# Down of both feed-forward blocks as seven products of quarter blocks, in a decoder layer on one Trainium2 core

## The chip, the cores and the metric

The kernel runs on one core of one Trainium2 chip. The core has five engines with an instruction queue each: TensorE (PE, matmuls; PEld is its loading of weights), VectorE (DVE), ScalarE (ACT), GpSimd (POOL) and SyncE (SP), which here issues most DMA transfers. Matmuls read on-chip memory (SBUF) and add up in PSUM, which has eight banks of 128x512 fp32. The metric is device time in microseconds (us), median of several runs; one further execution is recorded by the hardware profiler.

## The reference

One decoder layer on 1024 tokens of width 1024, all in fp32. A feed-forward block (ffn1), a token mixer and a second feed-forward block (ffn2) follow each other, each with a residual and a layer norm:

```
def swiglu(x, w_gate, w_up, w_down):
    return (jax.nn.silu(x @ w_gate) * (x @ w_up)) @ w_down

x = layer_norm(ALPHA * x + 0.5 * swiglu(x, ffn1_w_gate, ffn1_w_up, ffn1_w_down), ln1_g, ln1_b)
mix = token_mixer(x, ...)
x = layer_norm(ALPHA * x + mix, ln2_g, ln2_b)
x = layer_norm(ALPHA * x + 0.5 * swiglu(x, ffn2_w_gate, ffn2_w_up, ffn2_w_down), ln3_g, ln3_b)
```

The inner width of a feed-forward block is 2816 = 22 · 128. The token mixer (an mLSTM branch and an RWKV branch, merged by gates and multiplied by w_out) is left as it is.

## The kernel before

**Products.** Every fp32 product is made of three matmuls in a rounded fp32 format (`mm3`, L148): each operand is split into a high part (a cast on ACT, L131) and a low part (a subtraction on POOL or DVE, L135), and high·high, high·low and low·high are added in PSUM. A matmul has a 128x128 stationary and a 128x512 moving operand.

**Gate stage.** For each of the 22 blocks f of 128 inner columns, gate and up are made together as seven products of quarter blocks (`gate_up`, L272): four loads of weights (`rw`, a ring of 8 buffers), four subtractions between them (`weights`, L254; `tw` on DVE, L256), seven splits (ACT and POOL), 7·4·3 = 84 matmuls of 128x512 into three PSUM accumulators X, Y, Z (tags g, b, c), and additions on DVE that read PSUM (L277) and SBUF (L300, L304). The order of the seven is X, Y, X, Y, Z, Y, Z; what DVE reads of Y after the second product must be read before the fourth begins. h, the activated inner values, goes to DRAM in two stores per f (L285), with the inner dimension as rows and the tokens as columns. The first f of ffn1 (`gate_first`) also transposes x and makes its block sums (`put_sums`, L219) for four pairs of 128-token rows; pairs 0 and 1 before the first half of f = 0, pairs 2 and 3 between its two halves.

**Down stage.** `down_all` (L351) makes the 1024x1024 result in three passes over 128-token row blocks: 0 to 2, 3 to 5, 6 and 7. In each pass and for each f it loads a strip of h (`hr`, 128 x n·128) and two halves of a row block of w_down (`rw`), splits all three (ACT high, DVE low; split operands are in the ring `wr`), and runs 6n matmuls for n row blocks into the six or four accumulators of the pass. Half way through a pass the rows of x are loaded for the residual (tiles `u`, 128x1024, L378). At a pass's end DVE adds the accumulators to them (L386) and the rows are normalized (`layer_norm`, L396: statistics L399, centring on ACT L403, times g L404, a reciprocal root in small steps L161 to L165, times the root and plus b L413): those of passes one and two late, beside the next pass; rows 6 and 7 after the last matmul. At ffn1 each normalized row is also transposed on PE (L174) for the token mixer's products; at ffn2 it is the output. The same function makes w_out's product in the mixer (with 8 blocks instead of 22).

**What sets the order.** The kernel is written as a sequence of tile operations; a list scheduler of the framework orders each engine's instructions when the program is built. On the chip each engine works through its list in order and waits at an instruction whose inputs or buffers are not ready. SP too issues its DMAs in order, so a DMA that waits for a buffer holds up those behind it.

## Time and profile before

| | us |
|---|---|
| median of 3 runs | 3199.72 (3197.56 to 3206.72) |
| the profiled execution | 3204.13 |
| its span | 3202.1 |
| mean granted clock of PE in it | 0.977 |
| ffn1: first down matmul to last | 462.52 to 716.72 |
| ffn2: first down matmul to last | 2944.76 to 3187.88 |
| from ffn2's last down matmul to the end of the span | 14.2 |

All times of the profile are microseconds from the start of the span. Rows of the timeline and of groups name an engine, a line of the code and an operation as output<-inputs, with buffer numbers left out; `xN` counts instructions; in brackets stands how long the engine was idle before, and which instruction ended that. In the chain, which is followed back from the last instruction of the span, each row is a start, a duration and what took that time. Matmuls are pipelined, so the durations of single ones overlap; the chain's pieces do not.

### The profile page before, as it was taken

What the parts mean: (1) busy time and instruction counts of PE and PEld (TensorE: products, weight loads), DVE (VectorE), ACT (ScalarE), POOL (GpSimd) and SP (SyncE); (2) the same over time, 40 slices, a digit from 0 to 9 for tenths busy, and PEclk for the clock granted to TensorE, in tenths of its full rate; (3) what the DMA queues carried; (4) which work ended last, traced back from release to release, by engine and by line L of the source; (5) the groups of instructions that cost most, each with busy time, mean ns of one, the idle gap of its engine ahead of it and who ended that gap; (6) DMA issues with size and microseconds to landing.
All of it is one profiled execution on the core that took longest, in us unless ns stands there. A gap on an engine that the chain in (4) does not pass through costs nothing. (4 is left out here: it accounts for less than half of the span.)

```text
span 3202.1 us, 45591 instructions
## 1 busy us (share of the span) xinstructions
PE 3056.9 (95%) x15888; PEld 2486.7 (78%) x15888; DVE 1909.5 (60%) x4812; ACT 1098.2 (34%) x1836; POOL 761.8 (24%) x819
## 2 busy tenths in 40 slices
PE   7999999999899999999999999999999799999997
PEld 6888878877677777787877777777777688888886
DVE  7444435583657667758575856567648844444557
ACT  4333324453312222313131322186424433333444
POOL 4444420011212222222221222210000344442000
PEclk9999999999889999999999999999999899999999
DMA  4323236672222232322222323285586333223665
GB/s 128 97 83 86 79 107 215 200 220 72 64 54 77 69 77 60 80 56 75 68 72 64 85 67 99 70 273 175 171 270 196 102 87 89 83 86 112 215 202 186
DMA packets 497389, 373.81 MB, mean 117 GB/s; under 512 B 110941, under 2 KB 415751, under 8 KB 497159
## 3 DMA queue, kind: packets, MB, share of 16 engines
q1 hardware_dynamic: 488135, 357.26, 37.7%
q0 software_dynamic: 4608, 8.39, 1.0%
q10 hardware_dynamic: 4416, 5.24, 0.5%
q8 instruction: 125, 2.05, 0.3%
q14 instruction: 105, 0.86, 0.1%
HBM read 287.43 MB, written 83.36 MB: 116 GB/s over the span
## 5 line engine op out<-in xcount | busy, mean ns | idle before, releaser
L151 PE MATMUL psg<-xT,wf 128*128 128x512 f32 x2352 | 638.7, 408 | 1.6 <-DVE h L1108 0.9
L151 PEld LDWEIGHTS psg<-xT,wf 128*128 128x128 f32 x2352 | 428.0, 191 | 78.0 <-ACT wf L131 1.3
L131 ACT CAST wr<-rw 128x512 fp32r<-128x512 f32 x444 | 273.2, 621 | 489.8 <-PE psc L151 271.2
L135 DVE TENSOR_TENSOR wr<-rw,wr 128x512 fp32r<-128x512 f32 x312 | 215.6, 696 | 193.9 <-ACT wr L131 188.3
L151 PE MATMUL psa<-xT,w 128*128 128x512 f32 x1200 | 318.1, 407 | 7.5 <-DVE pj L480 4.7
L135 POOL TENSOR_TENSOR wr<-tw,wr 128x512 fp32r<-128x512 f32 x176 | 231.4, 1316 | 273.7 <-ACT wr L131 273.7
L135 POOL TENSOR_TENSOR wr<-rw,wr 128x512 fp32r<-128x512 f32 x132 | 175.9, 1333 | 432.8 <-DMA rw<-in_ffn_w_up_dram 239.2
L151 PEld LDWEIGHTS psa<-xT,w 128*128 128x128 f32 x1200 | 223.2, 192 | 59.3 <-DVE pj L480 9.4
L151 PE MATMUL psg<-wr,wr 128*128 128x512 f32 x936 | 250.8, 395 | 13.8 <-DVE wr L135 8.7
L151 PE MATMUL psb<-xq,wr 128*128 128x512 f32 (+1 forms) x1104 | 256.2, 381 | 4.7 <-DVE e L277 2.4
L151 PE MATMUL psc<-xq,wr 128*128 128x512 f32 (+1 forms) x1104 | 256.9, 380 | 1.6 <-POOL wr L135 1.6
L277 DVE TENSOR_TENSOR e<-psb,e 128x512 f32<-128x512 f32 (+1 forms) x138 | 92.1, 668 | 270.5 <-PE psb L151 270.5
L151 PE MATMUL psb<-wr,wr 128*128 128x512 f32 x936 | 247.2, 391 | 0.0
L151 PEld LDWEIGHTS psb<-xq,wr 128*128 128x128 f32 x1104 | 201.7, 188 | 45.5 <-issue 2.1
L151 PEld LDWEIGHTS psc<-xq,wr 128*128 128x128 f32 x1104 | 201.8, 188 | 41.5 <-POOL wr L135 1.8
L151 PEld LDWEIGHTS psg<-wr,wr 128*128 128x128 f32 x936 | 173.9, 188 | 58.9 <-DVE wr L135 16.2
L131 ACT CAST wr<-tw 128x512 fp32r<-128x512 f32 x176 | 108.9, 621 | 307.0 <-PE psb L151 217.9
L151 PEld LDWEIGHTS psb<-wr,wr 128*128 128x128 f32 x936 | 175.5, 188 | 36.3
L135 POOL TENSOR_TENSOR w<-raw,w 128x512 fp32r<-128x512 f32 (+1 forms) x51 | 65.5, 1297 | 488.3 <-ACT w L131 409.6
L135 POOL TENSOR_TENSOR wf<-rawf,wf 128x512 fp32r<-128x512 f32 x98 | 129.7, 1339 | 169.4 <-ACT wf L131 153.8
L151 PE MATMUL psc<-wr,wr 128*128 128x512 f32 x624 | 159.2, 390 | 0.0
L758 POOL TENSOR_SCALAR S<-S,PC 128x128 f32<-128x128 f32 x120 | 80.4, 670 | 292.8 <-DVE S L760 177.3
(345 smaller groups left out, 5104.5 us busy)
## 6 DMA issues: line engine op xcount, KB each, us to landing
rw<-in_ffn_w_down_dram SPq DMA_DIRECT2D x264, 256.0 KB
rawf<-in_w_in_dram SPq DMA_DIRECT2D x98, 256.0 KB
rw<-in_ffn_w_gate_dram SPq DMA_DIRECT2D x88, 256.0 KB
rw<-in_ffn_w_up_dram SPq DMA_DIRECT2D x88, 256.0 KB
h<-e SPq DMA_DIRECT2D x80, 256.0 KB
hr<-h SPq DMA_DIRECT2D x88, 192.0 KB
raw<-in_w_in_dram SPq DMA_DIRECT2D x50, 256.0 KB
rw<-in_w_out_dram SPq DMA_DIRECT2D x48, 256.0 KB
```

Of the source, the lines that this page charges most:

```text
L131: nc.scalar.copy(hi, src)
L135: eng.tensor_tensor(lo, src, hi.bitcast(F32), op=ALU.subtract)
L151: self.nc.tensor.matmul(out, a[u], b[v], start=first and i == 0, stop=last and i == 2, skip_group_check=more)
L277: add = lambda o, a, b: nc.vector.tensor_tensor(o, a[:, cs], b, op=ALU.add)
L758: nc.gpsimd.tensor_scalar(S1, S, pcn, None, op0=ALU.mult)
```

## The change

Down becomes seven products of quarter blocks. h (1024 tokens by 2816) and w_down (2816 by 1024) are each cut into 2x2 quarters; a product m goes over i = 0 to 10, a pair of 128-row blocks of the inner dimension, with a stationary of 128x512 (four token blocks) and a moving operand of 128x512, 12 matmuls per i. Four of the operands on each side are sums of quarters. These are made ahead, in the gate stage, by `sums`: for each i four loads of 128x512 (ring `pr`, 4 buffers), four DVE operations and four stores to DRAM. The sums of w are written into the program at f < 11, those of h at f > 11, when the h blocks that they need exist; the last of h stands at the start of `down_seven`. The products accumulate in three sets of four PSUM banks, X, Y, X, Z, Z, Y, Y; DVE adds each into the residual tiles at its end, twelve operations after the first product and four after each other one. All eight `u` tiles are loaded at i = 3 of the first product. Rows 0 to 3 are complete after the fifth product and normalized in the sixth and seventh; rows 4 to 7 after the seventh.

In `gate_first` the block sums of x of pairs 2 and 3 are put between the products of the first half of f = 0, two steps ahead of each. The constants of the token mixer (`consts2`) are loaded at the start of the sixth product rather than early in the first pass. The tiles `f` and `bnd3` of the mixer are no longer reserved during ffn1's down. `tw` has 5 buffers instead of 6, `wr` 12 in the down stages; w_out's product still goes through `down_all`.

```diff
-    RING = {"rw": (8, F32), "tw": (6, F32), "wr": (14, F32R), "e": (14, F32), "hr": (4, F32)}
+    RING = {"rw": (8, F32), "tw": (5, F32), "wr": (14, F32R), "e": (14, F32), "pr": (4, F32)}
...
+        def pr(ps, i, first):
+            for _ in range(2 if between and i else 0):
+                next(between, None)
+            self.prod(ps, ws[i], cmb[i], first, cs)
...
-        self.gate_up(cmb, 0, ws, hD, 0, 256)
-        pair(2)
-        pair(3)
+        steps = (s for p in (2, 3) for s in self.put_steps(cmb, p, *A[p], self.ring("tw"), "ad"))
+        self.gate_up(cmb, 0, ws, hD, 0, 256, steps)
+        for _ in steps:
+            pass
         self.gate_up(cmb, 0, ws, hD, 256, 512)
+        self.sums(pre, "w", self.I[f"{pre}_w_down"][0], 0)
...
+            if f < NH:
+                self.sums(pre, "w", wd, f)
+            elif f > NH:
+                self.sums(pre, "h", hD, f - NH - 1)
...
+    def sums(self, pre, kind, src, i):
...
+        q11, q12, q21, q22 = (self.ring("pr") for _ in range(4))
+        for t, r, c in ((q11, 0, 0), (q12, 0, 1), (q21, 1, 0), (q22, 1, 1)):
+            nc.sync.dma_start(t, self.quarter(src, kind, r, c, i))
+        if kind == "h":
+            tt_(q22, q21, q22, op=ALU.add)
+            tt_(q21, q11, q21, op=ALU.subtract)
+            tt_(q11, q22, q11, op=ALU.subtract)
+            tt_(q12, q12, q11, op=ALU.subtract)
+            out = q22, q11, q21, q12
+        else:
+            tt_(q11, q12, q11, op=ALU.subtract)
+            tt_(q12, q22, q12, op=ALU.subtract)
+            tt_(q22, q22, q11, op=ALU.subtract)
+            tt_(q21, q21, q22, op=ALU.subtract)
+            out = q11, q22, q12, q21
+        for m, t in enumerate(out):
+            nc.sync.dma_start(self.SD[key][(m * NH + i) * P:(m * NH + i + 1) * P, :], t)
...
+        self.parts = [(A(0, 0), B(0, 0)), (S(2), T(2)), (A(0, 1), B(1, 0)), (S(1), T(1)), (S(4), B(1, 1)),
+                      (S(3), T(3)), (A(1, 1), T(4))]
...
+    def down_seven(self, pre, src, hD, ln_cb, hooks, ahead):
...
+        self.sums(pre, "h", hD, NH - 1)
+        acc = {}
+        for m in range(7):
+            name = "XYXZZYY"[m]
+            first = m in (0, 1, 3)
+            if first:
+                acc[name] = [self.ps(t) for t in ("ggbb" if name == "Y" else "ccad")]
+            ps = acc[name]
+            for i in range(NH):
+                raws = ahead.pop(0) if ahead else self.part_load(m, i)
...
+                for t in raws:
+                    d = self.ring("wr"), self.ring("wr")
+                    self.split(t, *d, lo_eng="dve")
+                    ds.append(d)
+                if (m, i) == (0, 3):
+                    hooks[0]()
+                    for tt in range(8):
+                        t = self.unit()
+                        nc.sync.dma_start(t, src[tt * P:(tt + 1) * P, :])
+                        y.append(t)
+                if (m, i) == (5, 0):
+                    hooks[1]()
+                if i % 5 == 4 and late:
+                    late.pop(0)()
+                for j in range(4):
+                    self.mm3(ps[j], self.cut(ds[0], ALL, slice(j * P, (j + 1) * P)), ds[1], first and i == 0, i == NH - 1,
+                             not first)
+            for j in range(4):
+                c11, c12 = (y[j][:, c * 512:(c + 1) * 512] for c in range(2))
+                c21, c22 = (y[4 + j][:, c * 512:(c + 1) * 512] for c in range(2))
+                if m == 0:
+                    for t in (c12, c21, c22):
+                        stt(t, t, ALPHA, ps[j], op0=ALU.mult, op1=ALU.add)
+                elif m == 2:
+                    stt(c11, c11, ALPHA, ps[j], op0=ALU.mult, op1=ALU.add)
+                else:
+                    t = {1: c12, 3: c22, 4: c12, 5: c22, 6: c21}[m]
+                    tt_(t, t, ps[j], op=ALU.add)
+                if m == 4:
+                    late.append(lambda tt=j: ln_cb(tt, y))
+        for j in range(4):
+            ln_cb(4 + j, y)
```

Three places show what the scheduler makes of it. Lines of the changed kernel are its own: L396 to L399 are the four operations of a sum of w, L402 its stores, L447 the `u` loads, L418 the operands of the products, L466 an addition of a product to a residual tile, L523 to L537 the normalization; L291, L319, L323 and L269 are what L277, L300, L304 and L256 were.

SP at the start of ffn1's down, before (a strip of h and two halves of w_down are one f's operands):

```order
L346 DMA hr_4142<-h_77 128x384
L442 DMA vnat_3952<-in_m_conv_w_dram 64x128
L348 DMA rw_4143<-in_ffn_w_down_dram 128x512
L348 DMA rw_4144<-in_ffn_w_down_dram 128x512
L346 DMA hr_4178<-h_77 128x384
L378 DMA u_4232<-in_x_dram 128x1024
L378 DMA u_4234<-in_x_dram 128x1024
L348 DMA rw_4179<-in_ffn_w_down_dram 128x512
L348 DMA rw_4180<-in_ffn_w_down_dram 128x512
L346 DMA hr_4214<-h_77 128x384
L378 DMA u_4236<-in_x_dram 128x1024
```

The same queue now, from the stores of the last h sum to the fifth pair of operands of the first product (`rw_4238`, `rw_4239`):

```order
L402 DMA sum_ffn1h<-pr_4110 128x512
L402 DMA sum_ffn1h<-pr_4111 128x512
L447 DMA u_4210<-in_x_dram 128x1024
L447 DMA u_4212<-in_x_dram 128x1024
L447 DMA u_4214<-in_x_dram 128x1024
L447 DMA u_4216<-in_x_dram 128x1024
L447 DMA u_4218<-in_x_dram 128x1024
L447 DMA u_4220<-in_x_dram 128x1024
L447 DMA u_4222<-in_x_dram 128x1024
L447 DMA u_4224<-in_x_dram 128x1024
L418 DMA rw_4238<-h_77 128x512
L418 DMA rw_4239<-in_ffn_w_down_dram 128x512
```

The three `u` loads that stood among the operands are eight in a row, after the stores and ahead of the fifth pair.

DVE in the gate stage of ffn1, f = 3 from its second product on, before (`e` are the additions of the gate stage, `tw` the differences of weights for the next f):

```order
L277 TENSOR_TENSOR e_948<-psb_954,e_946 128x512
L256 TENSOR_TENSOR tw_1212<-rw_1208,rw_1204 128x512
L277 TENSOR_TENSOR e_949<-psb_954,e_946 128x512
L256 TENSOR_TENSOR tw_1213<-rw_1206,tw_1211 128x512
L277 TENSOR_TENSOR e_950<-psc_955,e_949 128x512
L256 TENSOR_TENSOR tw_1360<-rw_1354,rw_1352 128x512
L277 TENSOR_TENSOR e_951<-psb_954,e_946 128x512
```

The same stretch now (`pr` are the blocks of a sum of w):

```order
L291 TENSOR_TENSOR e_997<-psb_1003,e_995 128x512
L269 TENSOR_TENSOR tw_1292<-rw_1289,tw_1291 128x512
L396 TENSOR_TENSOR pr_1599<-pr_1600,pr_1599 128x512
L397 TENSOR_TENSOR pr_1600<-pr_1602,pr_1600 128x512
L291 TENSOR_TENSOR e_998<-psb_1003,e_995 128x512
L398 TENSOR_TENSOR pr_1602<-pr_1602,pr_1599 128x512
L269 TENSOR_TENSOR tw_1293<-rw_1289,rw_1285 128x512
L399 TENSOR_TENSOR pr_1601<-pr_1601,pr_1602 128x512
L291 TENSOR_TENSOR e_999<-psc_1004,e_998 128x512
L269 TENSOR_TENSOR tw_1294<-rw_1287,tw_1292 128x512
L291 TENSOR_TENSOR e_1000<-psb_1003,e_995 128x512
```

Between the readings of PSUM now stand the operations of a sum; a second sum follows in the same f, and f = 1 to 4 of ffn1 have two each.

DVE after the last product of ffn2, before:

```order
L386 SCALAR_TENSOR_TENSOR u_28380<-u_28380,psg_27967 128x512
L386 SCALAR_TENSOR_TENSOR u_28380<-u_28380,psg_27968 128x512
L399 BN_STATS lnst_28699<-u_28380 128x6 x2
L386 SCALAR_TENSOR_TENSOR u_28382<-u_28382,psb_27969 128x512
L400 BN_AGGR lnmv_28698<-lnst_28699 128x2
L386 SCALAR_TENSOR_TENSOR u_28382<-u_28382,psb_27970 128x512
```

And now:

```order
L466 TENSOR_TENSOR u_26730<-u_26730,psg_26930 128x512
L466 TENSOR_TENSOR u_26732<-u_26732,psg_26931 128x512
L523 BN_STATS lnst_28617<-u_26730 128x6
L466 TENSOR_TENSOR u_26734<-u_26734,psb_26932 128x512
L466 TENSOR_TENSOR u_26736<-u_26736,psb_26933 128x512
L524 BN_AGGR lnmv_28616<-lnst_28617 128x2
L523 BN_STATS lnst_28625<-u_26732 128x6
```

Two residual tiles were finished there, and now four are; 25 such rows of DVE stood from the first of these to the end of the program, and 49 stand there now.

More of the change, by code (lines that the diff above doesn't have):

```diff
@@ L22 @@
 NF = DFF // P
+NH = NF // 2
 ALPHA = 2.0 ** 0.25
@@ L225, in put_sums @@
         tt_(a2[0], a1[0], a2[0], op=ALU.subtract)
+        yield
         put(1, a1[1])
         tt_(a1[0], s1, a1[0], op=ALU.subtract)
+        yield
         put(2, a1[0])
+        yield
         put(3, a2[0])
         tt_(a1[1], a1[1], a1[0], op=ALU.subtract)
+        yield
         put(4, s1)
+        yield
         put(5, a2[1])
+        yield
         put(6, a1[1])
+    def put_sums(self, *args):
+        for _ in self.put_steps(*args):
+            pass
     def prod(self, ps, w, x, first, cs):
@@ L334, in gate_rest @@
             if f == NF - 1:
-                ahead = [self.row_load(wd, hD, 0, 3, i) for i in range(2)]
+                self.down_parts(pre, hD)
+                ahead = [self.part_load(0, i) for i in range(2)]
             if f == 0:
@@ new lines, in part_load @@
+    def part_load(self, m, i):
+        raws = [self.ring("rw") for _ in range(2)]
+        for t, part in zip(raws, self.parts[m]):
+            self.loaded = self.nc.sync.dma_start(t, part(i))
+        return raws
+    def down_seven(self, pre, src, hD, ln_cb, hooks, ahead):
+        nc = self.nc
+        stt, tt_ = nc.vector.scalar_tensor_tensor, nc.vector.tensor_tensor
+        y, late, ahead = [], [], list(ahead)
+        self.sums(pre, "h", hD, NH - 1)
[8 more added lines that the diff above has]
+                raws = ahead.pop(0) if ahead else self.part_load(m, i)
+                if (m, i) == (6, 6):
+                    self.held = self.loaded
+                ds = []
+                for t in raws:
[30 more added lines that the diff above has]
+            ln_cb(4 + j, y)
@@ L343, in row_load @@
     def row_load(self, wd, hD, t0, n, f):
-        hr, raws = self.ring("hr", n * P), [self.ring("rw") for _ in range(2)]
+        hr, raws = self.ring("pr", n * P), [self.ring("rw") for _ in range(2)]
         self.nc.sync.dma_start(hr, hD[f * P:(f + 1) * P, t0 * P:(t0 + n) * P])
@@ L372, in down_all @@
                     hook()
-                if (f % 3 == 2 if nf == NF else f % 2) and late:
+                if f % 2 and late:
                     late.pop(0)()
@@ L1169, in build @@
             gx.enter_context(net.shared("gx", ("xT",)))
-            gw.enter_context(net.shared("gw", [t for t in net.GLOBAL if t != "xT"]))
-            with net.phase("A", UB=6, side="right"):
+            gw.enter_context(net.shared("gw", ("raw", "w", "rawf", "wf")))
+            with net.phase("A", UB=8, side="right"):
                 net.wp = net.sp
-                net.down_all(ins["ffn1_w_down"][0], NF, x, h1, fin1, hook1, ahead)
+                net.down_seven("ffn1", x, h1, fin1, (hook1, net.consts2), ahead)
         middle(net, ins, x1T, x1D)
@@ L1202, in build @@
             xs.close()
-            with net.phase("F", UB=6, side="right"):
-                gb3.extend(rows("ln3"))
-                net.down_all(ins["ffn2_w_down"][0], NF, x2D, h2,
-                             lambda tt, y: net.layer_norm(tt, y, *gb3, lambda t: nc.sync.dma_start(out[0, row(t), :], y[t])),
-                             None, ahead)
+            with net.phase("F", UB=8, side="right"):
+                net.down_seven("ffn2", x2D, h2,
+                               lambda tt, y: net.layer_norm(tt, y, *gb3, lambda t: nc.sync.dma_start(out[0, row(t), :], y[t])),
+                               (lambda: gb3.extend(rows("ln3")), lambda: None), ahead)
         gx.close()
```

34 lines of the change are left out of this document (23 added, 11 removed).

## The prediction

> **What bounds the kernel now.** I read the page's busy shares first, then the chain of work that ended last, then tables of busy time by stage.
>
> ```profile
> PE 3056.9 (95%) x15888; PEld 2486.7 (78%) x15888; DVE 1909.5 (60%) x4812; ACT 1098.2 (34%) x1836; POOL 761.8 (24%) x819
> ```
>
> TensorE (PE) is busy 95% of the span, so matmuls set the time nearly everywhere. The table by stage shows where they do not (start:end, length, then busy time of PE, PEld, DVE, ACT, POOL, the granted clock, DMA share, GB/s):
>
> ```profile
> 7.00:55.00 48.00, 36.25 (x236) 32.84 (x237) 41.37 (x63) 23.55 (x43) 15.00 (x13) 0.93 0.47 143
> 80.00:400.00 320.00, 320.00 (x1413) 264.98 (x1412) 134.19 (x184) 100.09 (x168) 152.07 (x118) 1.00 0.30 86
> 470.00:500.00 30.00, 30.00 (x134) 24.48 (x133) 13.84 (x27) 11.60 (x21) 0.00 (x0) 1.00 0.85 284
> 462.52:716.72 254.20, 249.95 (x1106) 203.39 (x1107) 164.80 (x299) 121.60 (x222) 11.80 (x11) 0.99 0.68 215
> 2480.00:2540.00 60.00, 41.58 (x241) 33.20 (x242) 56.09 (x101) 24.76 (x42) 16.32 (x10) 0.86 0.34 109
> 2944.76:3187.88 243.12, 240.98 (x1057) 197.46 (x1055) 148.51 (x279) 109.40 (x198) 0.00 (x0) 1.00 0.64 210
> ```
>
> In the gate stage (80 to 400) PE has no idle time. The two down stages, 254.2 and 243.1 us, are PE-bound but for 4.3 and 2.1 us. The head (7 to 55) and the passage from w_out to the second gate stage (2480 to 2540) are VectorE's: DVE 41.4 of 48 and 56.1 of 60 us. The pace of a matmul is read from the chain, since the groups' means of 390 ns overlap:
>
> ```profile
> 2583.16 2.72 PE psg L151 x12
> ...
> 3182.45 1.36 PE psg L151 x6
> ```
>
> Both rows give 0.2267 us for one 128x512 matmul.
>
> **What the change removes.** Each ffn's down needs 8·2·22·3 = 1056 matmuls now and 7·11·4·3 = 924 afterwards. That is 264 fewer, 264 · 0.2267 = **-59.9 us**, all of it on the path. The sums are made against the profiled execution (3204.13 us, span 3202.1), 4.4 us above the median of 3199.72; the shift is then applied to the median.
>
> **What it adds: the eight u loads (+11, +5).** All rows of x are now loaded together early in the first product, ahead of the next operands in SP's queue; before, they went in threes between operands, half a pass in. These are the rows around the end of the first gate stage:
>
> ```profile
> 458.82 2.58 ACTq L285 DMA_DIRECT2D h<-e  x2
> ...
> 462.52 3.23 PE L151 MATMUL psg<-wr,wr 128*128 128x512 f32 x6 [3.13 <-ACT wr L131]
> ```
>
> PE idles 3.13 us before 462.52; call that idle time's start, 459.4, the gate stage's end, zero. The last h is issued by +2.0 (458.82 + 2.58). The last block sums need it, and behind them in SP's order stand their four stores, then the u loads, then the fifth pair of operands (i = 4). I use landings of 2.5 us after the issue, from the middle of these pieces of the chain (2.25 and 2.91 for loads; a store under load took 5.69):
>
> ```profile
> 2387.37 5.69 DMA mgD<-v
> ...
> 3125.53 2.25 DMA hr<-h
> ...
> 3136.22 2.91 DMA rw<-in_ffn_w_down_dram
> ```
>
> So h is in DRAM at +4.5, its four blocks are loaded at +8.5, the sums are done at about +12, and SP reaches the fifth pair at about +16. Ahead of it from +8 on are 4.2 MB of u, 1.0 MB of lng and lnb and 1.0 MB of stores. At the 284 GB/s of 470 to 500 they take 22 us. PE starts at +3.1 and has four pairs, 4 · 2.72 = 10.9 us of work: it needs the fifth at +14. If the pair landed 2.5 us after its issue, the wait would be 4 to 5 us; if all bytes go first at 284 GB/s, 16. I take **11**, nearer to the second, since the queue stands in that order. At ffn2 eight pairs (21.8 us) are loaded ahead and there is no gap before the stage: **5** (0 to 8).
>
> **The tails (+12, +9).** The left half of rows 4 to 7 gets its last part from the seventh product, so four rows are normalized after the last matmul, where two are now.
>
> ```profile
> 3185.88 1.37 DVE L386 SCALAR_TENSOR_TENSOR u<-u,psg 128x512 f32<-128x512 f32 x2 [2.23 <-PE psg L151]
> 3186.36 1.52 PE L151 MATMUL psb<-wr,wr 128*128 128x512 f32 x6
> 3187.17 1.28 DVE L399 BATCH_NORM_STATS2 lnst<-u 128x6 f32<-128x512 f32 x2
> ...
> 3193.03 0.16 DVE L164 SCALAR_TENSOR_TENSOR rst<-rst,lnv 128x2 f32<-128x2 f32 x1
> ...
> 3195.60 2.48 DVE L413 SCALAR_TENSOR_TENSOR u<-u,lnr,lnb 128x1024 f32<-128x1024 f32 x2
> 3196.92 1.54 SPq L1206 DMA_DIRECT2D out_dram<-u  x2
> ```
>
> Now DVE is dense from 3185.88 to 3198.08, 12.2 us. Afterwards stand four evictions (4 · 0.63), seven statistics (0.63 each), four final steps of 1.24 (L413, 2.48 for two), four products with g of the same size, and two root chains, 20 steps of 0.16 (0.2 with the gap behind each): 2.5 + 4.4 + 5.0 + 5.0 + 4 = 20.9, about 21. That is +9 at ffn2, hidden by nothing. At ffn1 the same rows are waited for by PE:
>
> ```profile
> 716.72 5.61 PE L151 MATMUL psg<-xT,wf 128*128 128x512 f32 x24
> ...
> 726.02 1.09 PE L174 MATMUL psa<-ident,u 128*128 128x128 f32 x4 [3.69 <-DVE u L413]
> ...
> 731.02 4.25 PE L151 MATMUL psa<-xT,w 128*128 128x512 f32 x15
> ```
>
> PE's order keeps the same 24 matmuls as cover and puts the transposes of all four rows before the next products: 9 of normalization and two more rows of transposes, about 2.5 each less overlap (726.02 to 731.02 for two), **+12** (8 to 14).
>
> **Block sums in the gate stage (+6, +6).** Each sum is four loads, four DVE subtractions of 128x512 and four stores. The order puts those of w at two per f for about four f's of each ffn; those of h come at one per f. What such an operation costs beside POOL (the first two rows are groups of 80 to 440, then the timeline):
>
> ```profile
> L277 DVE TENSOR_TENSOR e<-psb,e 128x512 f32<-128x512 f32 x57 | 39.4, 692 | 123.3 <-PE psb L151 123.3
> L304 DVE SCALAR_TENSOR_TENSOR e<-e,e 128x512 f32<-128x512 f32 x19 | 25.0, 1318 | 0.7
> ```
> ```profile
> 155.24 0.52 SPq L285 DMA_DIRECT2D h<-e  x1
> 155.30 1.30 POOL L135 TENSOR_TENSOR wr<-rw,wr 128x512 fp32r<-128x512 f32 x1 [1.41 <-ACT wr L131]
> 155.85 1.30 DVE L304 SCALAR_TENSOR_TENSOR e<-e,e 128x512 f32<-128x512 f32 x1
> 156.63 0.37 SPq L243 DMA_DIRECT2D rw<-in_ffn_w_gate_dram  x1
> ```
>
> L277 reads PSUM and takes 0.69. L304 reads SBUF twice, begins while POOL works (155.30 to 156.60) and ends only at 157.15: 0.55 us behind POOL's end. A sum costs 0.69 with POOL idle, 1.3 behind it, about 1.0 on average, since POOL is busy 152 of 320 us.
>
> [...]
>
> The `pr` ring has four buffers, one sum's worth, so sums form a loop: store issued (0.52), landed (2.5), two loads issued (0.74), landed (2.5), three subtractions (3.0), other DVE rows between (1.2): 10.5 us a turn. Two per f leave 84 · 0.2267 / 2 = 9.5. DVE takes its rows in order, so evictions wait behind a late sum, and PE behind them; an eviction has 2.0 us to spare (a product of 2.72 less 0.69). Eight turns 1 us too long, less 2 spare, make **+6** per ffn. Bounds: 8.5 a turn (2.25 landings, 0.69 a subtraction) costs nothing; 5.69 for the store and 1.77 a subtraction, as below, gives 16 and 50 per ffn. I stay by the load rows, which are 256 KB like these. The h sums, at one per f, have room: 0 (to 4).
>
> **The passage to ffn2 (+6).** Eight to ten w sums stand there among DVE's rows, where DVE is the bound.
>
> ```profile
> 2530.49 1.77 DVE L256 TENSOR_TENSOR tw<-rw,rw 128x512 f32<-128x512 f32 x1
> ```
>
> At 0.69 to 1.77 each they cost 6 to 17, less the 3.9 us in which DVE idles: 2 to 13, and 6 is nearest to the shorter rows, as POOL works only 16.3 of the 60.
>
> **The rest.** In the head the parts of x of pairs 2 and 3 move between products, which fills PE's gaps (48 - 36.3 us), and four sums are added to a busy DVE: -1 (-5 to +4). Evictions go from 16 to 36 per ffn, all but twelve between products on other banks; the twelve take 7.4 us against 6.8 of operands already split: about +1, and two fewer rows of transposes inside ffn1's down give that back. The normalization of rows 0 to 3 stalls PE as now (4.3 and 2.1 us of idle).
>
> **Sum:** -59.9 + 16 + 21 + 12 + 6 - 1 = **-5.9**: 3198 for the profiled execution, **3194** against the median.
>
> **Rivals.**
> *Faster: the loads and sums hide.* If a turn is below 9.5 us (landings at 2.25, subtractions finding POOL idle), the 12 us go; if the fifth pair lands soon after its issue, 8 of the 16. That gives 3194 - 20 = 3174. For it: DMA is at 0.30 of its share in the gate stage, and PE never waited there. Against it: the loop has no spare buffer.
> *Slower: the sums meet POOL.* If the three subtractions of a turn take 1.77 each, as at 2530.49, a turn is 12.8 us and each ffn loses 8 · 3.3 - 2 = 24 instead of 6: 3194 + 36 = 3230. It turns the sign from about 11.5 us a turn. For it: L304's row, and POOL as long busy as ever; against it: L256, also with two SBUF inputs, runs at 0.69 because it starts as POOL ends.
>
> ```profile
> L256 DVE TENSOR_TENSOR tw<-rw,rw 128x512 f32<-128x512 f32 x35 | 24.2, 692 | 39.6 <-POOL wr L135 39.6
> ```
>
> *The change doesn't do what it says:* the products run under the pace, for want of split operands. Each i needs two casts and two subtractions for twelve matmuls, where three of each stand now for 18; DVE is busy 165 of 254 us in the first down stage. So it could only happen where rows 0 to 3 are normalized beside it, in products six and seven. At 0.6 us lost in each of their 22 i's of both ffns it would be 26 us: 3220.
>
> **Chances.** Forecast 0.44 (3182 to 3206), faster rival 0.34, slower rival 0.18, pace 0.04. About 0.3%, 9.6 us, is what a measurement of this kernel can tell from no change; faster by more means below 3190.1, which is the faster rival and a fifth of the forecast's case: 0.43. Within: 0.36. Slower: 0.21. The range, 3164 to 3222, leaves out the lower end of the faster rival and more than half of the slower one, about 0.2.
>
> **What would show it.** Right: PE's pace of 1.36 per six in both down stages, which shrink by some 20 us each; one wait of PE for a DMA of rw some 14 us after each gate stage begins to be down; DVE dense for about 21 us after the last matmul; PE periods of about 21 us instead of 19.05 in four f's of each gate stage, DVE's L277 waiting behind sums that wait for DMA. Wrong: PE still 100% busy in 80 to 160, no wait at the fifth pair, or subtractions near 1.7 us. The term most likely to be mis-sized is the turn of the sums, then the u loads.

## The result, and the profile after

The changed kernel takes **3314.4 us** (median of 4 runs, 3314.08 to 3326.53) against 3198.64 (4 runs, 3197.05 to 3206.72): a ratio of **1.0354**, 95% interval 1.0333 to 1.0376. It is slower by 3.5%. The forecast was 3194 with a range up to 3222, so the time lies far outside, on the side that was given 0.21. The profiled executions are not the median ones: that of the changed kernel, with a span of 3324.7 us, is the slowest of its four, so 122.6 us more than in the profile before have to be found where the medians differ by 115.8.

Two rows of the page, the busy times and a group of PE by line and tile (matmuls of gate and up that go to the accumulator Y; ffn2 has further ones under another operand's name):

```profile
PE 3054.4 (92%) x15624; PEld 2474.3 (74%) x15624; DVE 2048.0 (62%) x4940; ACT 1067.3 (32%) x1750; POOL 778.6 (23%) x819
...
L154 PE MATMUL psb<-xq,wr 128*128 128x512 f32 (+1 forms) x1104 | 280.9, 406 | 63.8 <-DVE e L291 61.8
```

The 264 matmuls are gone (15888 to 15624), and yet PE is busy as long as before (3056.9): the matmuls that are left got slower, by some 57 us in all (an estimate: 3054.4 against 3056.9 less the 59.9 that 264 matmuls took). And the group of `psb` has 63.8 us of idle time before it, 61.8 of them ended by DVE's reading of PSUM (L291). Before, this was 4.7 us for the same 1104 matmuls. The table by stage (columns as in the prediction) shows the same:

```profile
80.00:400.00 320.00, 297.65 (x1263) 241.41 (x1262) 169.84 (x221) 90.56 (x152) 141.29 (x106) 0.97 0.51 157
2100.00:2200.00 100.00, 84.25 (x413) 66.66 (x412) 45.22 (x130) 43.58 (x66) 11.93 (x15) 0.91 0.56 175
```

From 80 to 400 PE was busy for all of the 320 us and made 1413 matmuls; now it makes 1263 and idles 22 us. The second row is a stretch of the token mixer, which the prediction had not looked at.

With marks that both traces have (the start of the last DVE operation of a block f of the gate stage, the first and last matmul of a stage) the 122.6 us divide as follows; the rows add up to 122.4, and f = 7 to 11 take 95.2 us in both. "Predicted" is the prediction's sum, put to the same stages.

| stage | before | after | difference | predicted |
|---|---|---|---|---|
| start to the end of f = 0, ffn1 | 64.3 | 61.2 | -3.1 | -1 |
| ffn1, f = 1 to 6 (w sums) | 110.6 | 131.6 | **+21.0** | +6 |
| ffn1, the last ten f (h sums) | 190.1 | 217.7 | **+27.6** | 0 |
| ffn1 down, from the gate stage's end to the last product | 257.3 | 245.7 | -11.6 | -19 |
| ffn1 tail, to the mixer's first product with `w` | 14.3 | 23.0 | +8.7 | +12 |
| mixer, to its last product | 1654.65 | 1690.19 | **+35.5** | 0 |
| passage, to the end of f = 0, ffn2 | 164.1 | 168.8 | +4.8 | +6 |
| ffn2, w sums | 110.7 | 131.0 | **+20.3** | +6 |
| ffn2, h sums | 190.41 | 220.66 | **+30.2** | 0 |
| ffn2 down | 243.1 | 225.1 | -18.0 | -25 |
| from ffn2's last product to the end | 14.2 | 21.1 | +6.9 | +9 |

The four rows of the sums are 99.1 us, the mixer 35.5; each of the others came out within 8 us of what was predicted. The first two rows are best read together, as 17.9 us: the kernel without sums (below) has the same head, and reaches the end of f = 11 only 0.2 us earlier than the kernel before (269.87 against 270.09). So the w sums of ffn1 cost about 18 us, and most of the 3.1 is a matter of where DVE's last operation of f = 0 happens to stand.

**The h sums.** What the engines waited for from 280 to 490 (us in total, times, longest):

```profile
DVE pr L390 <- DMA pr<-h: 27.2, 9, 4.6
...
PE psb L154 <- DVE e L291: 17.0, 9, 3.5
```

Nine f's, nine waits of DVE for the loaded h block, and nine waits of PE for DVE. One of them in the timeline (L304 stores h, L388 loads the blocks of a sum, L390 to L393 are the four operations of a sum of h, L402 its stores):

```profile
289.31 0.52 SPq L304 DMA_DIRECT2D h<-e  x1
292.63 1.84 SPq L388 DMA_DIRECT2D pr<-h  x3
...
297.60 2.88 PE L154 MATMUL psc<-xq,wr 128*128 128x512 f32 x12
297.81 0.69 DVE L390 TENSOR_TENSOR pr<-pr,pr 128x512 f32<-128x512 f32 x1 [2.90 <-DMA pr<-h]
298.53 1.67 DVE L391 TENSOR_TENSOR pr<-pr,pr 128x512 f32<-128x512 f32 x1
...
300.96 0.69 DVE L393 TENSOR_TENSOR pr<-pr,pr 128x512 f32<-128x512 f32 x1
301.57 0.68 DVE L291 TENSOR_TENSOR e<-psb,e 128x512 f32<-128x512 f32 x1
302.31 3.04 PE L154 MATMUL psb<-xq,wr 128*128 128x512 f32 x12 [1.83 <-DVE e L291]
```

Read it backwards. PE waits for L291 of 301.57, which reads Y after the fourth product. That product ends at about 297.6 (the next begins there), so DVE could have read it at 297.6. It does so 4 us later, because the four operations of the sum stand ahead of it, and they begin only at 297.81, when the load has landed. The load could not be issued before the last h store of the f before had landed (292.63), 3.3 us after that was issued; the sum that stands in f = 12 needs the block of f = 11, and when that is stored PE has been in f = 12 since 286.72. So in every f the chain store, load, four operations, reading, runs 302.25 - 289.31 = 12.9 us, and PE needs the reading after at most 11.2 (300.48, where its fifth product ends). PE loses 1.83 us, and then more: the ten f's last 21.8 us on average instead of 19.0; the rest is the clock, as will be seen under the hardware.

**The w sums.** What the engines waited for from 60 to 180:

```profile
DVE pr L396 <- DMA pr<-in_ffn_w_down_dram: 17.2, 5, 4.5
...
PE psb L154 <- DVE e L291: 14.3, 8, 3.8
```

Again DVE waits for the loads of a sum, and PE for DVE. In the chain of waits, pieces of two turns of the loop in ffn2 (start, duration, what took it):

```profile
2666.39 3.54 DMA sum_ffn2w<-pr
2669.95 4.92 DMA pr<-in_ffn_w_down_dram
...
2707.24 3.38 DMA sum_ffn2w<-pr
2710.64 4.30 DMA pr<-in_ffn_w_down_dram
...
2717.04 4.61 PE psb L154 x12
```

The loop is the one that the prediction described, the stores of one sum and the loads of the next through four buffers; it took 3.4 to 3.5 us for the store and 4.3 to 4.9 for the load.

**The first product.** SP, then PE, where the fifth pair of operands was late in ffn1:

```profile
518.93 4.08 SPq L447 DMA_DIRECT2D u<-in_x_dram  x8
523.13 0.63 SPq L418 DMA_DIRECT2D rw<-h  x1
...
534.56 3.23 PE L154 MATMUL psc<-wr,wr 128*128 128x512 f32 x6 [12.58 <-ACT wr L134]
```

In ffn2 the ninth pair is late by 11.97 us.

**The mixer.** PE in the stretch where the mLSTM chunks begin (`psg<-xT,wf` are large products that can run at any time, `psb<-qT,kT` a step of a chunk):

```profile
2129.66 21.24 PE L154 MATMUL psg<-xT,wf 128*128 128x512 f32 x93
...
2172.16 2.05 PE L1148 MATMUL psb<-qT,kT 128*128 128x128 f32 x16
```

In the trace of before the same stretch reads:

```profile
2082.26 11.38 PE L151 MATMUL psg<-xT,wf 128*128 128x512 f32 x49
2093.47 1.95 PE L1024 MATMUL psb<-qT,kT 128*128 128x128 f32 x16
```

Before, the large products ran between the chunks' steps, as cover for their waits. Now 93 of them run first, and the chunks afterwards with less beside them. In the two traces PE's order in the mixer, by names and shapes of the tiles, is the same for the first 7792 matmuls and for the last 382; what was reordered are the 1039 between. These are the two stretches, before and now (the first busy time is PE's):

```profile
2081.87:2297.62 215.75, 210.50 (x1039) 167.99 (x1040) 146.70 (x413) 141.63 (x210) 17.35 (x19) 1.00 0.64 201
2131.48:2375.49 244.01, 218.13 (x1040) 172.97 (x1039) 145.71 (x412) 144.82 (x213) 17.82 (x20) 0.96 0.60 181
```

PE idles 25.9 us instead of 5.3, and the stretch is 28.3 us longer. The other 7 of the 35.5 us lie in the 7792 matmuls ahead of it, whose order is the same and which take between 1342 and 1358 us in the twelve traces of this case: they are not the change.

### The profile page after: what moved, and what is told of

The parts are those of the page before. It is cut to its first block, busy times and chain, and to the rows that moved or that the text cites. A ratio compares the mean times of both kernels' runs of the same rounds, so it can differ in the third digit from the quotient of the medians.

```text
span 3324.7 us, 45401 instructions
## 1 busy us (share of the span) xinstructions
PE 3054.4 (92%) x15624; PEld 2474.3 (74%) x15624; DVE 2048.0 (62%) x4940; ACT 1067.3 (32%) x1750; POOL 778.6 (23%) x819
## 5 line engine op out<-in xcount | busy, mean ns | idle before, releaser
L134 ACT CAST wr<-rw 128x512 fp32r<-128x512 f32 x488 | 288.7, 621 | 521.9 <-PE psg L154 167.1
L138 DVE TENSOR_TENSOR wr<-rw,wr 128x512 fp32r<-128x512 f32 x356 | 237.2, 697 | 185.1 <-ACT wr L134 183.1
L154 PE MATMUL psb<-xq,wr 128*128 128x512 f32 (+1 forms) x1104 | 280.9, 406 | 63.8 <-DVE e L291 61.8
L138 POOL TENSOR_TENSOR wr<-tw,wr 128x512 fp32r<-128x512 f32 x176 | 242.9, 1382 | 356.5 <-ACT wr L134 348.4
L154 PEld LDWEIGHTS psb<-xq,wr 128*128 128x128 f32 x1104 | 213.0, 201 | 119.9 <-DVE e L291 75.1
L291 DVE TENSOR_TENSOR e<-psb,e 128x512 f32<-128x512 f32 (+1 forms) x138 | 91.7, 665 | 187.0 <-PE psb L154 187.0
L154 PE MATMUL psc<-wr,wr 128*128 128x512 f32 x624 | 164.4, 398 | 28.3 <-ACT wr L134 27.8
L154 PEld LDWEIGHTS psc<-wr,wr 128*128 128x128 f32 x624 | 118.8, 191 | 55.9 <-ACT wr L134 29.1
L154 PE MATMUL psg<-wr,wr 128*128 128x512 f32 x540 | 144.3, 396 | 7.6 <-DVE wr L138 6.9
L154 PE MATMUL psb<-wr,wr 128*128 128x512 f32 x540 | 143.9, 395 | 0.0
L134 ACT CAST wf<-rawf 128x512 fp32r<-128x512 f32 x122 | 73.4, 619 | 196.0 <-PE psg L154 117.0
```

Source lines behind the costliest of these rows:

```text
L134: nc.scalar.copy(hi, src)
L138: eng.tensor_tensor(lo, src, hi.bitcast(F32), op=ALU.subtract)
L154: self.nc.tensor.matmul(out, a[u], b[v], start=first and i == 0, stop=last and i == 2, skip_group_check=more)
L291: add = lambda o, a, b: nc.vector.tensor_tensor(o, a[:, cs], b, op=ALU.add)
```

## The experiments

A time without a number of runs is that of one execution, and the four of the changed kernel lie 12 us apart; so a difference of a few us is read from the stages of the traces, not from the time.

Three theories. **1:** the mixer's 35 us come from where the tiles `f` and `bnd3` are reserved: in the changed kernel their reservation opens and closes with the first phase of the mixer, before it spanned the whole mixer. **2a:** the 99 us of the gate stages come from order: DVE stands at an operation of a sum whose loads have not landed, and a reading of PSUM that PE waits for stands behind it. **2b**, its rival: they come from how much was added (sums on DVE, their conflicts with POOL, DMA traffic), wherever it stands. Such a conflict is the operation of 298.53 above: it lasts 1.67 us instead of 0.69 and ends 0.54 us behind a POOL operation of 298.33 to 299.66. The `u` loads' 12.6 and 12.0 us are a separate point.

**Undo one thing: the reservation of `f` and `bnd3`.** `middle_in` holds the rest of `middle` unchanged.

```diff
-    with net.shared("gf", ("f", "bnd3")), net.phase("B", VB=4):
+    with net.shared("gf", ("f", "bnd3")):
+        middle_in(net, ins, x1T, x1D)
+
+def middle_in(net, ins, x1T, x1D):
+    nc, tc = net.nc, net.tc
+    with net.phase("B", VB=4):
```

> The pool of the tiles f and bnd3 stays open through the whole token mixer, as in the kernel before, and no longer closes with the mixer's first phase; all else is the changed kernel. Theory 1 (the pool's early end makes the mixer's next phase wait for the side work that still uses f): the stretch from the branch products' first reading of xT to the end of w_in's products loses the 34 us that it gained, 3314 becomes about 3280. Rival (the new stretch of idle PE there comes from another order of the scheduler or from the constants being loaded later): 3305 to 3315.

3279.71 (before on that chip: 3204.25), 34.7 us less than the changed kernel's median. PE's order in the whole mixer is that of the kernel before again, and so is the length of the stretch:

```profile
2122.32:2338.40 216.08, 211.19 (x1039) 167.43 (x1040) 147.02 (x413) 141.44 (x210) 17.34 (x19) 1.00 0.65 201
```

PE's rows in the program of this kernel, with + where they stand at this place only here, against the changed kernel:

```
 L154 MATMUL psg_10126<-xT_5650,wf_10116 128x512
+L1084 MATMUL psb_19137<-ident,v_19135 128x128 x4
 L154 MATMUL psg_10126<-xT_5649,wf_10117 128x512
...
 L154 MATMUL psg_10192<-xT_5650,wf_10182 128x512
+L1148 MATMUL psb_19148<-qT_19122,kT_19123 128x128 x8
+L1156 MATMUL psb_19159<-ident,kT_19123 128x128 x4
 L154 MATMUL psg_10192<-xT_5649,wf_10182 128x512
```

So theory 1 holds: with a reservation that ends with a phase, the scheduler put the next phase's steps behind that phase's large products. What this costs doesn't hang on one execution: the five traces with the old order (before, this one, and the three kernels below that contain this edit) need 215.8 to 216.3 us for the stretch, the seven with the new one 240.9 to 244.4, some 25 to 29 us more. Which rule of the scheduler does this was not looked into, and the reverse edit on the kernel before was not tried.

**Leave the sums out.** All calls of `sums` are removed and the products that need sums read plain quarters instead; the result is another one, the number and size of the matmuls and of the products' loads are unchanged.

> All block sums are left out, loads, DVE operations and stores; the products that should read sums read plain quarters of h and w_down, so the output is another. Theory 2 (the gate stages lose 41 us by the sums of w and 58 by those of h): both gate stages are back at 19.05 us a period, 3314 becomes about 3210. If the gate stages lose their time to something else in the change (the smaller tw ring, the shared buffers), they stay slow and the time stays above 3280.

3181.60. The gate stage is what it was before the change, to the second decimal of PE's row:

```profile
80.00:400.00 320.00, 320.00 (x1413) 264.98 (x1412) 134.20 (x184) 100.05 (x168) 151.68 (x119) 1.00 0.30 84
```

That is 132.8 us less, more than the 99 of the gate stages: with no last h sum ahead of them in SP's order, the `u` loads are early enough as well: the longest waits of PE in the first products are 3.24 us (ffn1, at the stage's start) and 3.49 us (ffn2). The reordered stretch of the mixer still takes 241.4 us. This says that the sums cost the 99 us, not by which of the two ways.

**Take away the loads of the sums.** Four blocks are loaded once per sort of sum and changed in place 11 times; the sums are other numbers, DVE's operations and the stores are as many as before.

```diff
         if key not in self.SD:
             self.SD[key] = self.dram("sum_" + key, 4 * NH * P, 512)
-        q11, q12, q21, q22 = (self.ring("pr") for _ in range(4))
-        for t, r, c in ((q11, 0, 0), (q12, 0, 1), (q21, 1, 0), (q22, 1, 1)):
-            nc.sync.dma_start(t, self.quarter(src, kind, r, c, i))
+            self.held4 = tuple(self.ring("pr") for _ in range(4))
+            for t, r, c in zip(self.held4, (0, 0, 1, 1), (0, 1, 0, 1)):
+                nc.sync.dma_start(t, self.quarter(src, kind, r, c, i))
+        q11, q12, q21, q22 = self.held4
```

> The sums' DVE operations and stores stand as in the changed kernel, but their four blocks are loaded once per kind and ffn and then changed in place again and again, so the output is another; the loads are gone, the DVE work is not. Theory 2a (PE loses because DVE, which works in order, stands at a sum whose loads have not landed): the gate stages lose under 5 us per ffn on w and under 10 on h, about 3235. Theory 2b (the additional DVE work itself, and its exclusion with POOL, is too much): the periods stay at 21 to 24 us, 3295 to 3315.

3250.01, between the two. It doesn't decide, since the scheduler, with no loads to wait for, packed three and four sums into one f. In the first of these f's (27.6 us) DVE is nearly full, and PE waits for it with no DMA in play (the table by stage, then the waits from 60 to 130):

```profile
60.00:87.60 27.60, 22.80 (x89) 18.28 (x88) 25.62 (x32) 6.15 (x11) 11.08 (x8) 0.88 0.68 222
```
```profile
PE psb L154 <- DVE e L291: 10.8, 3, 4.8
```

So an amount can stop PE too, at three or four sums in an f. The changed kernel has two at most, where 2b is still open.

**The same work in another place.** One sum in each f (w at f = 1 to 11, h at 12 to 21); its loads are written ahead of the f's products, its operations may issue only after the addition that follows the fifth product.

```diff
-        add(up1, Z, u3)
+        at = add(up1, Z, u3)
+        if mid:
+            with self.tc.issue_after(at.ins):
+                mid()
         pr(Y, 5, False)
...
-                self.gate_up(cmb, f, ws, hD)
-            if f < NH:
-                self.sums(pre, "w", wd, f)
-            elif f > NH:
-                self.sums(pre, "h", hD, f - NH - 1)
+                kind, src, i = ("w", wd, f - 1) if f <= NH else ("h", hD, f - NH - 1)
+                q = self.sum_load(pre, kind, src, i)
+                self.gate_up(cmb, f, ws, hD, mid=lambda: self.sum_make(pre, kind, q, i))
```

> The same sums with the same loads and stores, but one per f (w at f = 1 to 11, h at f = 12 to 21), the loads ahead of the f's products and the four DVE operations held behind the addition that follows the fifth product. Theory 2a: the loads have 14 us to land, so DVE never stands at a sum; periods of 19.05 to 19.5 us, about 3225. Theory 2b: the same DVE work at an even rate costs about as much in all, 2 us in every period, 3290 to 3310.

3210.74, 103.7 us less than the changed kernel. PE is full, with DVE busy 202 us where it was 170 in the changed kernel's slower stage, and with a larger DMA share (0.63 against 0.51):

```profile
80.00:400.00 320.00, 320.00 (x1414) 264.96 (x1413) 202.11 (x251) 97.23 (x167) 168.53 (x118) 1.00 0.63 193
```

The same stretch of an h sum in its timeline (L391 here is the load, L401 to L404 the operations):

```profile
289.22 0.53 SPq L304 DMA_DIRECT2D h<-e  x1
292.55 1.29 SPq L391 DMA_DIRECT2D pr<-h  x3
296.12 0.69 DVE L291 TENSOR_TENSOR e<-psb,e 128x512 f32<-128x512 f32 x1 [2.90 <-PE psb L154]
...
299.45 1.76 DVE L401 TENSOR_TENSOR pr<-pr,pr 128x512 f32<-128x512 f32 x1
...
304.04 0.68 DVE L291 TENSOR_TENSOR e<-psb,e 128x512 f32<-128x512 f32 x1
```

Store and load take as long as before (289.22, 292.55), the first operation even lasts 1.76 us, but the reading of `psb` that PE waits for (296.12) now stands ahead of them, and there DVE waits for PE (2.90 us), not PE for DVE. Since w was also thinned from two to one per f, this run by itself decides for the h sums only; the next one covers the rest.

**The same pace, but early.** As above, with the operations behind the addition after the second product (two readings earlier).

```diff
-        add(u2, Y, p1)
+        at = add(u2, Y, p1)
+        if mid:
+            with self.tc.issue_after(at.ins):
+                mid()
```

> As e4_paced, one sum per f, but its four DVE operations are held behind the addition after the second product instead of the fifth, which is where the changed kernel has those of h. Theory 2a (waiting for loads): the loads of w, free to go a whole f earlier, have landed, so the first eleven periods stay at 19.05 us; those of h cannot go before the store of the f before, so DVE stands some 3 us at each and these ten periods are 21 to 25 us as in the changed kernel: about 3270. Theory 2b (DVE work): as e4_paced in both halves, about 3211. Were the place in the row bad in itself, both halves would be slow: about 3300.

3267.39: theory 2a. The amount per f is the same as in the kernel before this one, and half of the experiment shows no loss: the w sums, whose loads need nothing that the f makes, leave PE full (180 of 180 us). The h sums, whose loads wait for the store of the f before, cost PE 18 us in 200:

```profile
80.00:260.00 180.00, 180.00 (x796) 149.10 (x795) 117.30 (x141) 56.61 (x95) 87.53 (x67) 1.00 0.62 193
280.00:480.00 200.00, 181.86 (x763) 146.79 (x762) 105.62 (x130) 51.44 (x86) 80.86 (x60) 0.97 0.52 163
```
```profile
DVE pr L401 <- DMA pr<-h: 33.9, 10, 5.9
...
PE psb L154 <- DVE e L291: 18.1, 9, 3.5
```

It is not the work, then, but its standing, unready, ahead of something that PE needs: the ten f's of h last 219.2 and 215.0 us here, and 187.9 and 188.4 in the kernel before this one. For the w sums one point stays open: whether two per f, well placed, would also have been free.

**Spread the `u` loads** over i = 3 to 10 of the first product, one at a time (and `lng`, `lnb` at the third product), on the changed kernel.

```diff
-                if (m, i) == (0, 3):
+                if (m, i) == (2, 0):
                     hooks[0]()
-                    for tt in range(8):
-                        t = self.unit()
-                        nc.sync.dma_start(t, src[tt * P:(tt + 1) * P, :])
-                        y.append(t)
+                if m == 0 and i > 2:
+                    t = self.unit()
+                    nc.sync.dma_start(t, src[(i - 3) * P:(i - 2) * P, :])
+                    y.append(t)
```

> The changed kernel with its eight u loads spread over the first product, one at each of i = 3 to 10, so that each stands behind one pair of operands in SP's queue; lng and lnb are loaded at the start of the third product. Theory 3 (PE waits 12.6 and 12.0 us at the fifth and ninth pair because 4 MB of u go first): both waits fall below 3 us, and with the lower clock behind them gone 3314 becomes about 3288. Rival (the waits come from the last sum of h, which stands in the same place): they stay above 8 us, 3305 to 3314.

3304.85, 9.6 less instead of 26. The wait at the fifth pair is down to 0.94 us, but another stands at the start of the second product:

```profile
554.09 2.50 PE L154 MATMUL psg<-wr,wr 128*128 128x512 f32 x5 [6.75 <-DVE wr L138]
```

Just ahead of it DVE has the twelve additions of the first product, from 545.57 to 552.75 without a break, so they no longer wait for their `u` tiles. The splits of the second product's operands stand behind them. What is left here is therefore not the loads, but twelve additions at once at the product's end; by the stages, ffn1's down got 9.9 us shorter and ffn2's 1.9.

**The three edits together** (reservation, pace, spread).

> The three edits together on the changed kernel: the mixer's pool open throughout, one sum per f behind the fifth product's addition, the u loads spread. If the causes are separate their gains add: 104 + 34 + about 20 off 3314, 3155 to 3160, 1.3% faster than the kernel before. If spread loads and sums get in each other's way at the start of down, 3170 to 3176.

3178.95 (5 runs, 3170.22 to 3191.7) against 3203.12: 0.9927, interval 0.9902 to 0.9952. It is 0.7% faster than before the change, but misses the expected 3155 to 3160 by some 20 us; PE still idles 6.75 and 6.97 us at the start of the second product of each ffn.

**The same without the parts of x between the first products** (`gate_first` as before the change).

> e7_three with the block sums of x of pairs 2 and 3 back where they were, between the two halves of f = 0. In the changed kernel the head ended 3.1 us earlier than before with four sums of w in it; without sums the interleaving may be worth more. Theory: 3 to 6 us slower than e7_three. Rival (the head is bound by DVE, whose work is the same): within 1 us of it.

3185.99 (5 runs, 3179.02 to 3197.08): 0.9952, interval 0.9928 to 0.9977. The two intervals overlap, so this part is worth 7 us only by the medians, and the traces don't bear them out. DVE's last operation of f = 0 begins 2.5 us later (62.78 against 60.31), but by the end of f = 11 the two kernels are 0.5 us apart (270.42 against 269.95), as the rival had it. What the profiled executions differ by lies mostly in the mixer, where PE's order is the same in both and takes 1645.7 and 1657.5 us. A gain of more than 1 us by this part is not shown.

**Loads of `u` from i = 6 of the first product, additions two per i of the second.** First in addition to the three edits:

```diff
+                if 6 <= m * NH + i < 14:
+                    n = m * NH + i - 6
+                    tt = n // 2 + 4 * (n % 2)
+                    y[tt] = self.unit()
+                    nc.sync.dma_start(y[tt], src[tt * P:(tt + 1) * P, :])
+                for _ in range(2 if m == 1 and i else 0):
+                    if wait0:
+                        wait0.pop(0)()
...
+                if m == 0:
+                    for r, c in ((0, 1), (4, 0), (4, 1)):
+                        def ev(r=r, j=j, c=c, p=ps[j]):
+                            t = y[r + j][:, c * 512:(c + 1) * 512]
+                            stt(t, t, ALPHA, p, op0=ALU.mult, op1=ALU.add)
+                        wait0.append(ev)
+                    continue
```

> e7_three with the u loads two thirds of a product later (one at each of the steps i = 6 of the first product to i = 2 of the second, rows 0, 4, 1, 5, ... in turn) and the twelve additions of the first product taken two at each i of the second product instead of in one row. In e7_three PE waited 6.7 and 7.0 us at the start of the second product for splits that stood in DVE's row behind these additions, and DMA was at 0.99 of its share beside the first product. Theory 3a (a crowd on DMA and DVE at the end of the first product): both waits vanish and the first product's stalls shrink, 3179 becomes 3160 to 3166. Rival (the operands of the second product come late for another reason, the last sum of h): the waits stay, 3175 to 3182.

**3159.95** (4 runs, 3152.36 to 3162.8) against 3205.69: **0.9866**, interval 0.9849 to 0.9882. This beats both kernels, the one before by 1.3%. Its gate stage and its first product:

```profile
60.00:440.00 380.00, 380.00 (x1678) 314.63 (x1678) 238.17 (x296) 117.14 (x200) 200.33 (x140) 1.00 0.61 191
455.00:490.00 35.00, 31.40 (x131) 25.29 (x130) 19.99 (x32) 14.39 (x25) 0.00 (x0) 0.95 0.90 317
```

Of the 3.6 us in which PE idles from 455 to 490, 3.29 are the start of the stage, which was there before the change (3.13). Then the same `u` edit alone on the changed kernel:

> The changed kernel with the u loads and the additions of the first product as in e9_defer, and nothing else: sums and the mixer's pool as changed. It gives the price of the u loads by themselves, where e5_spread had 9.5 us with its twelve additions still in one row. Theory 3a: the waits of 12 us at the fifth and ninth pairs, and those that took their place in e5_spread, are gone: 3314 becomes about 3288. If the loads were only moved from one wait to another, it stays near 3305.

3286.16, 28.2 us less than the changed kernel: so much did the eight loads and the twelve additions together cost, in both ffn's. In the traces the two down stages are 21.6 and 14.9 us shorter, and no wait of PE above 1 us is left in their first two products but the one at ffn1's start.

## Why the prediction was wrong

The mechanism of the gain was right, and several terms were. What failed are three steps, by size of what they missed:

1. **"The h sums, at one per f, have room: 0 (to 4)"** failed, by 27.6 and 30.2 us. The step counted the turn of the loop against the length of an f. It did not ask what stands behind the waiting operation. A loop that turns in time can still start late in every f: its load cannot leave until the h store of the f before has landed, when PE is already in the next f, and the readings of PSUM wait behind it. The prediction had said of the w sums that "DVE takes its rows in order, so evictions wait behind a late sum"; the same sentence held for h. Shown by the early and the paced kernel, which differ in this place alone.
2. **"The rest", where the token mixer was not priced**, failed by 35.5 us in the profiled execution, of which 28.3 are the change. The text ahead of the prediction names the shorter reservation of `f` and `bnd3`; the sum has no term for it, and no reason why not. It reorders PE for a stretch of 244 us. Shown by the first experiment (-34.7) and by the stretch's length in all twelve traces.
3. **The turn of the w sums (+6 per ffn)** had the right loop and the wrong size: +21.0 (about 18 of it theirs, as said at the table) and +20.3. Predicted was a turn of 10.5 us with landings of 2.5 us after the issue, so 3.0 for a store and 3.2 for two loads. The chain shows 3.4 to 3.5 and 4.3 to 4.9, and f = 1 to 4, with two sums each, last 23.5 us on average over both ffn's, that is 11.8 a turn. By the prediction's own formula, 8 turns 2.3 us too long, less 2, are 16. The landings had been taken from pieces of the trace where DMA had less to do (a share of 0.57 from 3120 to 3140 there, 0.69 to 0.77 beside the w sums now). For all 88 loads of each sort, the page has these medians from issue to landing (the last column), beside the weights' loads:

```profile
rw<-in_ffn_w_gate_dram SPq DMA_DIRECT2D x88, 256.0 KB, 3.0
...
pr<-in_ffn_w_down_dram SPq DMA_DIRECT2D x88, 256.0 KB, 4.2
pr<-h SPq DMA_DIRECT2D x88, 256.0 KB, 3.7
```

The other terms, in order:

- **The matmuls (-59.9)**: right. 264 are gone and the pace of six in about 1.36 us stands where nothing waits; PE's six of 3300.76 in the last product are followed by the next six at 3302.11. Down in ffn1 and ffn2 got shorter by 11.6 and 18.0 with their waits of 12.6 and 12.0 us in them. In the best kernel, without those waits, the two stages (last gate matmul to last down matmul) take 226.1 and 212.8 us, 31.4 and 30.2 less than before: 61.6.
- **The `u` loads (+11, +5)**: too low in sum. The first wait was right (12.58), with its mechanism: SP reached the fifth pair 18 us after the gate stage's end (523.13 against 504.9; predicted 16), and it landed late, 10.0 us after its issue, behind the `u` bytes. The second was 11.97: the cover of eight pairs was counted, but the last h sum was late by itself, and SP reached the ninth pair 23 us after the stage's first matmul. Both together cost more than the two waits, 28.2 us by the last experiment against 16, which includes the twelve additions (+1 in the prediction, 2.64 us of waiting in ffn1).
- **The tails (+12, +9)**: right, a little high: +8.7 and +6.9. In ffn1 PE idles 6.30 us for the first normalized row, after its cover of 24 matmuls:

```profile
750.62 5.61 PE L154 MATMUL psg<-xT,wf 128*128 128x512 f32 x24
762.53 1.09 PE L177 MATMUL psa<-ident,u 128*128 128x128 f32 x4 [6.30 <-DVE u L537]
```

- **The passage (+6)** measured +4.8: right. **The head (-1)** measured -3.1 at the end of f = 0, but by the end of f = 11 the kernels with this head and no wait up to there (without sums, early, paced, and those built on the paced one) are 0.2 to 1.2 us ahead of the kernel before: about as predicted.
- **The rival that the products run under the pace**: did not happen. Beside the two `u` waits PE waits for more than 1 us three times in the two down stages, all in ffn1: 3.29 at the start, 2.64 at the second product and 3.59 at 743.73, for the copy of a transposed row.
- **The slower rival** named the right place and the right sign, and a wrong mechanism: operations of 1.77 us beside POOL. The medians of all eight kinds of operations lie at 0.69, as in this one's row (least, median, most in ns):

```profile
L390 DVE TENSOR_TENSOR pr<-pr,pr x22: 691/693/1810, 297.8 to 3091.8; 128x512 f32<-128x512 f32 x22
```

It was the waiting for loads that stretched the turn past the 11.5 us which that rival gave for the change of sign (by the prediction's own terms its sum is nothing at 10.9 us; at 11.5 it is slower by more than the 9.6 us that can be told from no change). The lower bound of 8.5 us a turn adds up to 9.0 by its terms, which costs nothing either.

So the idea is worth what its matmuls say, less the tails and the passage: with the order put right, the two down stages gain 61.6 us in the trace, and the best kernel is 45.7 us faster than the one before.

## What to carry to other kernels

An operation that waits for a DMA costs what stands behind it in its engine's order, not its own duration; ask of every such operation added whether a reading that the critical engine needs comes next, and put it behind that reading (the same four operations cost nothing after the fifth product, and 27 to 31 us per ffn two readings earlier). When a load needs a store of the iteration just before, count the chain store, load, use from the moment of the store, not the throughput of the loop. And price every line of a diff that changes where buffers are reserved by looking at the order of the phases that use them, however far from the change they are.

## What the runs showed of the hardware

**A short wait can cost more than itself, and the clock's record says when.** The twelve matmuls behind a wait usually take 2.88 to 3.04 us, but some groups behind a wait of the same length take over 4:

```profile
323.46 4.21 PE L154 MATMUL psb<-xq,wr 128*128 128x512 f32 x12 [1.79 <-DVE e L291]
370.67 3.02 PE L154 MATMUL psb<-xq,wr 128*128 128x512 f32 x12 [1.79 <-DVE e L291]
```

The granted clock explains the two. In these traces its records are at 1.00 or 0.50, and the stretches at 0.50 begin at times that are multiples of 3.41 us apart. The first wait lies within one such interval, which has 1.79 us of idle PE, and the clock is 0.50 in the next. The second is cut by a boundary at 369.36 into 0.48 and 1.31 us, and the clock stays:

```profile
321.58:324.99 3.41, 1.62 (x8) 1.28 (x8) 3.38 (x5) 0.57 (x1) 1.70 (x1) 1.00 0.62 221
324.99:328.40 3.41, 3.41 (x10) 2.67 (x9) 1.38 (x3) 0.62 (x1) 0.37 (x1) 0.50 0.66 166
369.36:372.77 3.41, 2.10 (x9) 1.75 (x10) 3.41 (x5) 0.01 (x1) 1.71 (x1) 1.00 0.79 263
372.78:376.18 3.40, 3.40 (x17) 2.82 (x16) 1.40 (x3) 1.26 (x2) 1.29 (x1) 1.00 0.46 124
```

It comes out the same throughout the gate stages of all twelve traces. Of the intervals at clock 1.00, 74 are followed by one at 0.50, and each of these has at least 1.75 us of idle PE; the other 2845 have at most 1.80. In the changed kernel's trace alone (60 to 504.9 and 2560 to 3060) these are 15 with at least 1.79 us and 235 with at most 1.71. Other stages, with smaller matmuls, were not worked out. So in these stages it took idle time of about half an interval, 1.75 to 1.80 of 3.41 us, and where a wait of 1.79 us fell decided whether it cost 1.2 us more (4.21 against 3.02).

The granted clock in stretches with such waits is 0.91 (2100 to 2200) to 0.97 (80 to 400), and 1.00 in the kernels without them; over the whole span it is 0.955, against 0.977 before. The group of `psb` alone has a mean of 406 ns (381 before) in 1104 matmuls, 27.6 us. Without the waits the slow matmuls are gone as well: PE is busy for 2995.5 us in the best kernel, where 3056.9 - 59.9 = 2997.0 were to be expected.

**A load's landing depends on when it runs.** Loads of 256 KB had medians of 3.0 us (weights), 3.7 and 4.2 us (sums) in one kernel; the operand behind the `u` loads in ffn2 took 9.61 us in the chain, with a DMA share of 0.99 from 3100 to 3120.
